# Grouped attention in a decoder trunk: the weighted sums in two products, with values' main part and remainder side by side

## The chip, the cores and the metric

The kernel runs on one core of a Trainium2 chip. The metric is the device time of one execution in microseconds (us); lower is better. A core has a matrix engine (TensorE, PE in the profile, with its weight loads shown as PEld), a vector engine (VectorE, DVE), a scalar engine (ScalarE, ACT), GpSimd (POOL) and SyncE (SP). TensorE writes its results to PSUM; the other data lie in SBUF. Both are memories of 128 partitions, and an instruction works on the same columns of many partitions at once.

## The reference

The reference is a decoder trunk of four layers over 256 positions of width 2048. Each layer normalizes its input, projects it, mixes the positions, multiplies by a gate, projects back and adds. The mixers cycle: latent attention, sparse attention over selected keys, sliding-window attention with sinks, latent attention again. The change touches the second and the third, which both are grouped: 32 query heads share 4 key and value heads, 8 to a group, of width 64. Cut to the lines that matter:

```python
# sparse layer (selected keys)
s = jnp.einsum('bqgjd,bqkgd->bqgjk', qb, kg, preferred_element_type=jnp.float32) * B_HEAD_DIM ** -0.5 + bias
p = jax.nn.softmax(s, axis=-1)
return jnp.einsum('bqgjk,bqkgd->bqgjd', p.astype(vg.dtype), vg)
...
# sliding-window layer
s = jnp.einsum('bqgjd,bkgd->bgjqk', qb, kb, preferred_element_type=jnp.float32) * scale + bias
p = e / (jnp.sum(e, axis=-1, keepdims=True) + jnp.exp(sink - m))
return jnp.einsum('bgjqk,bkgd->bqgjd', p.astype(vb.dtype), vb)
...
# both
y = jnp.concatenate([self_out, mem_out], axis=-1) * jax.nn.silu(gate)
x = x + y @ w_out[i]
```

The last `einsum` of each mixer is the weighted sum of values. All inputs are 32-bit floats.

## The kernel before

**Numbers in two parts.** Most matrix products are done on a rounded 32-bit type (`F32R`). To keep accuracy an operand is split into a main part and a remainder: `split` (L67) lets ScalarE copy the value into the rounded type (L60) and VectorE subtract that copy from the value (L69). A product of two split operands is three matmuls: main by main, main by remainder, remainder by main.

**The projections.** Weights come from memory by SyncE's queue into buffers `wr`; `parts_of` (L233) splits each 512-column piece into `wh` and `wl`, with three buffers of each. `rows_by` (L239) uses such a piece in six products of 512 columns (L264, L265, L266, for two row blocks), `columns_by` (L269) in four of 512 (L284) and four of 256 (L288). ScalarE makes `wh`, VectorE `wl`, TensorE uses both.

**Order.** The program is written as one sequence. A scheduler that simulates the engines decides in which order each engine gets its instructions, under the data dependencies; each engine then runs its own list strictly in order and waits on semaphores. A few instructions are pinned to the written order. Tiles with the same tag share a fixed number of buffers. PSUM tiles from `misc` (tag `mp`) share four; the score tiles `sp`, the transposed weights `tp`, the indexer's tiles and the sums `o` are among them.

**Grouped attention.** `Grouped.first` projects keys and values and, in the sliding-window layer, calls `spaced_values` at once. In the sparse layer an indexer (`select`, `stacked_late`, `selection`) runs first, in steps between other work, and `spaced_values` follows at its end. `stacked_late` contains, at L841 and L843, a copy from the upper to the lower half of the partitions on ScalarE and an addition on VectorE.

`spaced_values` (L766) writes the values of the four groups, 64 columns each, into two zeroed tiles `vz[0]` (main part, tag `big1`) and `vz[1]` (remainder, tag `big2`) of 9 x 64 columns per key block, with 64 zero columns between them. GpSimd zeroes them (L772).

`Grouped.attend` (L902) works on one group of 8 heads in the order 0, 2, 1, 3, 4, 6, 5, 7. For each head two query blocks of 128 are scored, put through a softmax and transposed: three 128 x 128 blocks, since the first query block sees one key block and the second sees two. The transposed weights are split into `pHL[0]` and `pHL[1]`. Two even heads (or two odd heads) fill one such pair of tiles. After the second of them come the weighted sums (L940), called one event here: for key block `t` = 0, 512 columns of weights (two blocks of two heads), for `t` = 1, 256 columns, and for each the three products. The 128 columns of `vz` that serve as the other operand begin at the values for even heads and 64 columns earlier for odd heads, so that the sums of even heads land in partitions 0 to 63 and those of odd heads in 64 to 127, and zeros are added to the other half. The even and the odd event add into one PSUM tile `o`. After the odd one VectorE multiplies `o` by the gate (L946) into `yt`, a tile of a kind with three buffers, and `yt` is split into `y`.

A layer runs its parts in the order 4, 0, 1, 2, 3, 5 (4 and 5 are attention to the memory); the output projection `w_out` of a part is written after the next part's attention. One layer has 4 groups with 4 events each.

Of the kernel before, what the change touches and what calls it, by code (L numbers as in the profile page):

```python
# [9 lines left out]
F32R = mybir.dt.float32r  # L10
I32 = mybir.dt.int32
AF = mybir.ActivationFunctionType
# [3 lines left out]
P = 128  # L16
S = 256
# [14 lines left out]
def kernel(ctx: ExitStack, tc: tile.TileContext, a: dict, out: bass.AP,  # L32
                             kinds=(0, 1, 2, 0)):
    nc = tc.nc
# [3 lines left out]
    act = ctx.enter_context(tc.tile_pool(name="act", bufs=1))  # L38
# [4 lines left out]
    def misc(name, dt=F32):  # L43
        return ps.tile([P, 512], dt, name=name, tag="mp", bufs=4)

    def tmp(name, n=512, dt=F32):
        return wk.tile([P, n], dt, name=name, tag=f"t{n}", bufs=3)
# [5 lines left out]
    def f32(ap):  # L53
        return ap.bitcast(F32)
# [4 lines left out]
    def copy_act(o, i, scale=1.0):  # L59
        inst = nc.scalar.activation(o, i, AF.Copy, scale=scale)  # L60
        if pinned:
            tc.keep_in_program_order(inst)
# [4 lines left out]
    def split(hi, lo, src):  # L67
        copy_act(hi, src)
        nc.vector.tensor_sub(lo, src, f32(hi))  # L69
# [158 lines left out]
    def other_work():  # L228
        for _ in range(2):
            if steps and next(steps[0], None) is None:  # L230
                steps.pop(0)
# [268 lines left out]
    def attend(o, v, pT):  # L500
        nc.tensor.matmul(o, v[0], pT[:, :S], start=True, stop=False)
        nc.tensor.matmul(o[:, P:], v[1], pT[:, S:S + P], start=False, stop=True)
# [109 lines left out]
    class Latent:  # L612
# [101 lines left out]
        def attend(self, qn, qr, kn, v, gT):  # L714
            y = act.tile([P, 2, 4, S], F32R, name="y", tag="y", bufs=2)
            for h in range(4):
                def score(b):
                    sp = misc("sp")
                    qs = slice(b * P, (b + 1) * P)
                    q, k, z = qn[h // 2], kn[h // 2], h % 2  # L720
                    if b == 0:
                        seq = [(q[:, 0, z, qs], k[:, :, z, :P]), (q[:, 1, z, qs], k[:, :, z, :P]),
                               (qr[:, h, qs], self.kr[:, :, :P])]
                    else:
                        seq = [(q[:, 0, z, qs], k[:, 0, z, :]), (q[:, 0, z, qs], k[:, 1, z, :]),
                               (q[:, 1, z, qs], k[:, 0, z, :]),
                               (qr[:, h, qs], self.kr[:, 0, :]), (qr[:, h, qs], self.kr[:, 1, :])]
                    for n_, (l, r_) in enumerate(seq):
                        nc.tensor.matmul(sp[:, :S], l, r_, start=n_ == 0, stop=n_ == len(seq) - 1)
                    return sp  # L730
                tp = masked_softmax(score, lambda b, n: caus[:, S - n:], self.scale)
                pT = wk.tile([P, 768], F32, name="pT", tag="pT", bufs=PT)[:, :512]
                copy_act(pT[:, :3 * P], tp[:, :3 * P])
                if h % 2 == 0:
                    o = misc("o")
                attend(o[:, (h % 2) * S:(h % 2 + 1) * S],
                       [v[:, t, h * P:(h + 1) * P] for t in range(2)], pT)
                if h % 2 == 1:
                    gated(y, o, gT, h - 1)
            return y  # L740


    class Grouped:
# [22 lines left out]

        def spaced_values(self):


            self.vz = [act.tile([P, 2, 9 * 64], F32R, name="vz", tag=f"big{1 + z}") for z in range(2)]  # L770
            for z in range(2):
                nc.gpsimd.memset(f32(self.vz[z]), 0.0)  # L772
            for t in range(2):
                hi, lo = (self.vz[z][:, t, 64:].rearrange("p (g c) -> p g c", c=P)[:, :, :64] for z in range(2))
                split(hi, lo, self.v[:, t, :].rearrange("p (g c) -> p g c", c=64))

        def dup(self, dst, src, sc, n):

# [123 lines left out]
        def attend(self, g, q, bm, gT):  # L902
            while steps:
                other_work()
            y = act.tile([P, 2, 4, S], F32R, name="y", tag="y", bufs=2)
            for h in (0, 2, 1, 3, 4, 6, 5, 7):
                def score(b):
                    sp = misc("sp")
                    qb = q[h // 4][:, h % 4, b * P:(b + 1) * P]
                    if b == 0:  # L910
                        nc.tensor.matmul(sp[:, :S], qb, self.k[:, g, :, :P], start=True, stop=True)
                    else:
                        for v in range(2):
                            nc.tensor.matmul(sp[:, :S], qb, self.k[:, g, v, :],
                                             start=v == 0, stop=v == 1)
                    return sp

                def bias(b, n):
                    bh = bm[:, h, S - n:]
                    if not self.sparse:  # L920
                        return bh
                    bs = wk.tile([P, S], F32, name="bs", tag="e", bufs=4)
                    nc.vector.tensor_add(bs[:, :n], bh, self.sel[:, b, :n])
                    return bs[:, :n]
                nsk = None if self.sparse else nsink[:, g * 8 + h:g * 8 + h + 1]
                tp = masked_softmax(score, bias, None, nsk)

                half, odd = h // 2 % 2, h % 2
                if half == 0:
                    pHL = [wk.tile([P, 3, 2, P], F32R, name="pT2", tag="pT", bufs=PT) for z in range(2)]  # L930
                split(pHL[0][:, :, half, :], pHL[1][:, :, half, :],
                      tp[:, :3 * P].rearrange("p (i c) -> p i c", i=3))
                if half == 0:
                    continue
                if not odd:
                    o = misc("o")
                v0 = g * P + (0 if odd else 64)
                for t in range(2):
                    for n_, (z, p_) in enumerate(((0, 0), (0, 1), (1, 0))):
                        nc.tensor.matmul(o[:, t * S:], self.vz[z][:, t, v0:v0 + P],  # L940
                                         pHL[p_][:, 2 * t:2 + t].rearrange("p i h c -> p (i h c)"),
                                         start=odd == t == n_ == 0, stop=odd == t == 1 and n_ == 2)
                if odd:
                    j = (h // 4) * 2
                    yt = tmp("yt")
                    nc.vector.tensor_mul(yt.rearrange("p (j b c) -> p j b c", j=2, b=2),  # L946
                                         o.rearrange("p (b j c) -> p j b c", b=2, j=2),
                                         gT[:, j:j + 2, :].rearrange("p j (b c) -> p j b c", b=2))
                    split(y[:, 0, j:j + 2, :], y[:, 1, j:j + 2, :], yt.rearrange("p (a b) -> p a b", a=2))
            return y  # L950

# [129 lines left out]
```

## Time and profile before

| | |
|---|---|
| runs of the kernel | 2596.93, 2597.0, 2600.05 us; median 2597.0 |
| the profiled execution | 2597.13 us |
| its span, first to last instruction | 2595.3 us |
| mean granted TensorE clock | 0.998 |
| bytes moved by DMA | 509.53 MB |
| matmuls | 14066 |

The profile is one execution, recorded by the hardware. Its page gives the busy time of each engine, the span in 40 slices, the chain of work that ended last, and the costliest groups of instructions. A group's row names line, engine, operation, tiles (output, arrow, inputs), shape and count; behind the bar stand the busy time in us, the mean duration of one in ns, and the idle time of the engine just before, with what ended it. Further views of the same execution give the waits, a timeline, or busy times by windows. Durations of matmuls that follow each other overlap, so the time that one takes from the span is the distance between starts.

### The profile page before, as it was taken

To read this page: it belongs to the slowest core of one execution; us is meant where nothing else is said; L and a number is where in the kernel's file an instruction comes from. 1 tells how busy PE (TensorE), PEld (TensorE's weight loads), DVE (VectorE), ACT (ScalarE), POOL (GpSimd) and SP (SyncE) were. 2 spreads that over 40 slices of the span, in tenths; PEclk is the share of its full clock that TensorE was granted. 3 is DMA by queue.
4 is the path that set the end of the run, shared out by engine and by line. 5 is a ranking of instruction groups with operands and counts; after the bars stand their busy time and mean duration, and the time that the engine had idled before them with its cause. 6 is when DMAs were issued, how large, how long until landed. Compare 5 with 4: busy or idle time off the path is not lost.

```text
span 2595.3 us, 41702 instructions
## 1 busy us (share of the span) xinstructions
PE 2576.4 (99%) x14066; PEld 2216.7 (85%) x14066; DVE 1880.5 (72%) x4130; ACT 1619.6 (62%) x3420; POOL 68.0 (3%) x124
## 2 busy tenths in 40 slices
PE   9999999999999999999999999999999999999997
PEld 7888898888888888888888888888888888888886
DVE  7666667667776686787778776777778767676667
ACT  6556556556656566667666666676666655665655
POOL 0100000000000010000000000000000000000000
PEclk9999999999999999999999999999999999999999
DMA  7888777666676667566556575555655766566664
GB/s 257 254 258 267 242 214 234 185 171 190 193 203 201 197 218 246 163 196 189 192 164 199 170 224 170 175 174 180 195 161 149 233 183 168 170 167 182 212 178 131
DMA packets 455128, 509.53 MB, mean 196 GB/s; under 512 B 68816, under 2 KB 351712, under 8 KB 453760
## 3 DMA queue, kind: packets, MB, share of 16 engines
q1 hardware_dynamic: 441392, 449.58, 57.9%
q0 software_dynamic: 13088, 56.16, 6.8%
q8 instruction: 110, 1.80, 0.3%
q10 hardware_dynamic: 432, 1.11, 0.1%
q14 instruction: 106, 0.87, 0.1%
HBM read 487.81 MB, written 31.56 MB: 200 GB/s over the span
## 4 chain that ended last, share of the span: by engine, by line
PE 99%; DVE 1%; ACT 0%; DMA 0%; SPq 0%; issue 0%; ACTq 0%
PE acc_g L284 14%; PE acc_g L288 7%; PE acc_wo L264 7%; PE acc_wo L265 7%; PE acc_wo L266 7%; PE acc_mk L284 5%; PE acc_mq L284 5%; PE acc_cq L284 3%; PE acc_qn L284 3%; PE acc_mq L288 2%; PE acc_mk L288 2%; PE acc_q L265 2%; PE acc_q L266 2%; PE acc_q L264 2%; PE acc_mv L265 2%; PE acc_mv L264 2%
## 5 line engine op out<-in xcount | busy, mean ns | idle before, releaser
L69 DVE TENSOR_TENSOR wl<-wr,wh 128x512 fp32r<-128x512 f32 (+2 forms) x1728 | 1165.0, 677 | 625.8 <-ACT wh L60 602.8
L60 ACT ACTIVATE wh<-wr 128x512 fp32r<-128x512 f32 (+2 forms) x1728 | 1070.4, 621 | 813.8 <-PE acc_g L284 179.3
L284 PE MATMUL acc_g<-xT,wh 128*128 128x512 f32 x1536 | 486.3, 396 | 0.0
L288 PEld LDWEIGHTS acc_g<-xT,wl 128*128 128x128 f32 x1536 | 284.8, 188 | 60.8
L288 PE MATMUL acc_g<-xT,wl 128*128 128x256 f32 x1536 | 310.5, 280 | 0.0
L265 PE MATMUL acc_wo<-wl,y 128*128 128x512 f32 x768 | 303.5, 395 | 0.2 <-DVE wl L69 0.2
L266 PE MATMUL acc_wo<-wh,y 128*128 128x512 f32 x768 | 298.2, 390 | 0.0
L284 PEld LDWEIGHTS acc_g<-xT,wh 128*128 128x128 f32 x1536 | 238.3, 189 | 4.4
L264 PE MATMUL acc_wo<-wh,y 128*128 128x512 f32 x768 | 240.1, 391 | 0.1
L265 PEld LDWEIGHTS acc_wo<-wl,y 128*128 128x128 f32 x768 | 144.3, 188 | 28.4 <-DVE wl L69 0.6
L266 PEld LDWEIGHTS acc_wo<-wh,y 128*128 128x128 f32 x768 | 144.3, 188 | 27.9
L264 PEld LDWEIGHTS acc_wo<-wh,y 128*128 128x128 f32 x768 | 142.2, 188 | 29.2 <-ACT y L60 1.0
L284 PE MATMUL acc_mk<-mT,wh 128*128 128x512 f32 x512 | 161.7, 396 | 0.3 <-DVE mv L418 0.3
L284 PE MATMUL acc_mq<-xT,wh 128*128 128x512 f32 x512 | 161.6, 396 | 0.0
L968 DVE TENSOR_TENSOR x<-x,acc_wo 128x512 f32<-128x512 f32 x192 | 126.1, 681 | 5.7 <-PE acc_wo L266 5.6
L284 PE MATMUL acc_qn<-cT,wh 128*128 128x512 f32 x384 | 121.2, 397 | 0.0
L284 PE MATMUL acc_cq<-xT,wh 128*128 128x512 f32 x384 | 120.8, 396 | 0.0
L288 PEld LDWEIGHTS acc_mk<-mT,wl 128*128 128x128 f32 x512 | 96.0, 188 | 22.3 <-DVE wl L69 0.4
L288 PEld LDWEIGHTS acc_mq<-xT,wl 128*128 128x128 f32 x512 | 94.0, 188 | 20.1
L288 PE MATMUL acc_mq<-xT,wl 128*128 128x256 f32 x512 | 103.3, 282 | 0.0
L288 PE MATMUL acc_mk<-mT,wl 128*128 128x256 f32 x512 | 101.9, 278 | 0.0
L265 PE MATMUL acc_q<-wl,xT 128*128 128x512 f32 x256 | 101.1, 395 | 0.0
(304 smaller groups left out, 4272.5 us busy)
## 6 DMA issues: line engine op xcount, KB each, us to landing
wr<-in_w_out_dram SPq DMA_DIRECT2D x192, 512.0 KB, 3.6
wr<-in_w_in_a_dram SPq DMA_DIRECT2D x176, 512.0 KB, 4.0
wr<-in_w_mem_kv_dram SPq DMA_DIRECT2D x120, 512.0 KB, 4.4
wr<-in_w_in_b_dram SPq DMA_DIRECT2D x112, 512.0 KB, 3.5
wr<-in_w_in_c_dram SPq DMA_DIRECT2D x104, 512.0 KB, 3.5
wr<-in_w_uq_dram SPq DMA_DIRECT2D x192, 128.0 KB, 2.5
wr<-in_w_uq_dram SPq DMA_DIRECT2D x48, 256.0 KB, 3.7
tab<-flat POOLq DMA_DIRECT2D x8, 1536.0 KB, 9.4
```

Source lines behind the costliest of these rows:

```text
L60: inst = nc.scalar.activation(o, i, AF.Copy, scale=scale)
L69: nc.vector.tensor_sub(lo, src, f32(hi))
L264: nc.tensor.matmul(acc[t][:, :n], xh, wh[:, :n], start=first, stop=False)
L265: nc.tensor.matmul(acc[t][:, :n], xh, wl[:, :n], start=False, stop=False)
L266: nc.tensor.matmul(acc[t][:, :n], xl, wh[:, :n], start=False, stop=last)
L284: nc.tensor.matmul(acc[j], wh[:, o:o + P], q[:, :, kt % 4, :], start=kt == 0, stop=False)
L288: nc.tensor.matmul(acc[j][:, 0, :], wl[:, o:o + P], q[:, 0, kt % 4, :], start=False, stop=kt == kts - 1)
L968: nc.vector.tensor_add(xs, xs, acc[t])
```

## The change

The diff touches `spaced_values` and the end of `Grouped.attend`.

- There is one tile of spaced values, in tag `big2`. A group has 192 columns: 64 zeros, the 64 values' main parts, their 64 remainders.
- An event has two products for each key block. The first multiplies the main part of the weights by the columns main, remainder: partitions 0 to 63 get main by main, 64 to 127 get remainder by main. The second multiplies the remainder of the weights by the columns zeros, main: it adds main by remainder into partitions 64 to 127.
- Each event has its own tile `o`. The two halves are added across partitions: ScalarE copies the other half of `o` into this head pair's half of `yt`, and VectorE adds this half of `o`. Even heads end in partitions 0 to 63 of `yt`, odd heads in 64 to 127, as before.
- The product with the gate reads `yt` and writes `yt`, where it read `o`.

```diff
         def spaced_values(self):
 
-
-            self.vz = [act.tile([P, 2, 9 * 64], F32R, name="vz", tag=f"big{1 + z}") for z in range(2)]
-            for z in range(2):
-                nc.gpsimd.memset(f32(self.vz[z]), 0.0)
-            for t in range(2):
-                hi, lo = (self.vz[z][:, t, 64:].rearrange("p (g c) -> p g c", c=P)[:, :, :64] for z in range(2))
-                split(hi, lo, self.v[:, t, :].rearrange("p (g c) -> p g c", c=64))
+            self.vz = act.tile([P, 2, 4 * 192], F32R, name="vz", tag="big2")
+            nc.gpsimd.memset(f32(self.vz), 0.0)
+            for t in range(2):
+                v3 = self.vz[:, t, :].rearrange("p (g c) -> p g c", c=192)
+                split(v3[:, :, 64:128], v3[:, :, 128:], self.v[:, t, :].rearrange("p (g c) -> p g c", c=64))
...
                 if half == 0:
                     continue
+
+
+                o = misc("o")
+                for t in range(2):
+                    for p_ in range(2):
+                        c0 = g * 192 + 64 * (1 - p_)
+                        nc.tensor.matmul(o[:, t * S:], self.vz[:, t, c0:c0 + P],
+                                         pHL[p_][:, 2 * t:2 + t].rearrange("p i h c -> p (i h c)"),
+                                         start=t == p_ == 0, stop=t == p_ == 1)
                 if not odd:
-                    o = misc("o")
-                v0 = g * P + (0 if odd else 64)
-                for t in range(2):
-                    for n_, (z, p_) in enumerate(((0, 0), (0, 1), (1, 0))):
-                        nc.tensor.matmul(o[:, t * S:], self.vz[z][:, t, v0:v0 + P],
-                                         pHL[p_][:, 2 * t:2 + t].rearrange("p i h c -> p (i h c)"),
-                                         start=odd == t == n_ == 0, stop=odd == t == 1 and n_ == 2)
+                    yt = tmp("yt")
+                here, other = (slice(64, P), slice(0, 64)) if odd else (slice(0, 64), slice(64, P))
+                oj = o.rearrange("p (b j c) -> p j b c", b=2, j=2)
+                yj = yt.rearrange("p (j b c) -> p j b c", j=2, b=2)
+                nc.scalar.activation(yj[here], oj[other], AF.Copy)
+                nc.vector.tensor_add(yj[here], yj[here], oj[here])
                 if odd:
                     j = (h // 4) * 2
-                    yt = tmp("yt")
-                    nc.vector.tensor_mul(yt.rearrange("p (j b c) -> p j b c", j=2, b=2),
-                                         o.rearrange("p (b j c) -> p j b c", b=2, j=2),
-                                         gT[:, j:j + 2, :].rearrange("p j (b c) -> p j b c", b=2))
+                    nc.vector.tensor_mul(yt, yt, gT[:, j:j + 2, :].rearrange("p a b -> p (a b)"))
                     split(y[:, 0, j:j + 2, :], y[:, 1, j:j + 2, :], yt.rearrange("p (a b) -> p a b", a=2))
```

## The prediction

> **What bounds the kernel now.** I read the page first: the busy times, the clock in the slices, the chain that ended last.
>
> ```profile
> span 2595.3 us, 41702 instructions
> ## 1 busy us (share of the span) xinstructions
> PE 2576.4 (99%) x14066; PEld 2216.7 (85%) x14066; DVE 1880.5 (72%) x4130; ACT 1619.6 (62%) x3420; POOL 68.0 (3%) x124
> ...
> PEclk9999999999999999999999999999999999999999
> ...
> PE 99%; DVE 1%; ACT 0%; DMA 0%; SPq 0%; issue 0%; ACTq 0%
> ```
>
> TensorE (PE) is busy for 99% of the span at full clock, and 99% of the chain is matmuls. A busy PE need not be a PE at its limit, because matmuls overlap. So I asked next where the changed products lie, then what PE waited for in that stretch, then how loaded the other engines are there. The first row below is the tile view of the spaced values (shortest, median, longest ns; first and last start). The next six are all of PE's waits over the span (us in total, times, longest); cut to 1160 to 1940 us, the same view keeps the rows of `o` and `acc_wo` alone. The last two are windows that hold one layer's changed products each: length, then busy time of PE, PEld, DVE, ACT and POOL, clock, DMA share, GB/s.
>
> ```profile
> L940 PE MATMUL o<-pT,vz x192: 277/336/496, 1163.5 to 1936.8; 128*128 128x512 f32 x96, 128*128 128x256 f32 x96
> ```
>
> ```profile
> PE spr L175 <- DVE dg L174: 2.6, 1, 2.6
> PE wu L101 <- DVE ones L97: 1.1, 1, 1.1
> PE acc_mv L264 <- ACT wh L60: 1.1, 2, 0.6
> PE o L940 <- DVE pT L69: 0.3, 1, 0.3
> PE acc_mk L284 <- DVE mv L418: 0.3, 1, 0.3
> PE acc_wo L265 <- DVE wl L69: 0.2, 1, 0.2
> ```
>
> ```profile
> 1160.00:1545.00 385.00, 384.76 (x2062) 327.83 (x2061) 300.91 (x702) 256.92 (x576) 10.89 (x17) 1.00 0.60 188
> 1620.00:1940.00 320.00, 319.60 (x1705) 270.86 (x1705) 245.34 (x614) 218.39 (x533) 3.79 (x5) 1.00 0.57 178
> ```
>
> In 780 us PE waited 0.5 us. VectorE (DVE) has 84 and 75 us free in the two windows, ScalarE (ACT) 128 and 102 us. Here the number of matmul columns sets the time, so columns taken out come off the span unless what replaces them makes PE wait.
>
> **The products that go.** The grouped view gives the number of products by form; a piece of the chain holds one event whose six products stand together, and what follows them.
>
> ```profile
> L940 PE MATMUL o<-pT,vz 128*128 128x512 f32 x96 | 32.5, 400 | 0.3 <-DVE pT L69 0.3
> L940 PE MATMUL o<-pT,vz 128*128 128x256 f32 x96 | 16.5, 280 | 0.0
> L940 PEld LDWEIGHTS o<-pT,vz 128*128 128x128 f32 x192 | 33.2, 188 | 6.5 <-DVE pT L69 0.8
> ```
>
> ```profile
> 1182.41 1.05 PE o L940 x6
> 1183.46 0.46 PE acc_q L264 x2
> ```
>
> The 192 products are 32 events of six (2 layers, 4 groups, 4 pairs of heads): three of 512 columns, three of 256. The change leaves two of each, so 64 products go, with their weight loads. The means of 400 and 280 ns overlap and are not the price. The chain is: six take 1.05 us, from 1182.41 to the next product at 1183.46. A 512-column product takes 0.46 / 2 = 0.23 us there, which leaves (1.05 - 3 x 0.23) / 3 = 0.12 us for one of 256. An event loses 0.23 + 0.12 = 0.35 us, 32 events lose 11.2 us. A weight load takes 188 ns and yet these products follow each other after 0.12 us, so loads overlap and add nothing to the price.
>
> The Trainium skill gives, for a stream of weight loads and matmuls in a real kernel, about 81 ns a matmul at 128 columns and 131 ns at 512 (TensorE: Matmul & The Clock Gate, Back-to-back issue gap). By that, as an estimate, an event would lose between 0.131 + 0.081 and 0.131 + 0.131 us, and the sum would be 6.8 to 8.4 us. The row of 1.05 us for six disagrees: by the page's figures six would take 0.64 to 0.79 us.
>
> **What comes in.** Each event now ends in a ScalarE copy of 64 x 512 out of PSUM, from the other half of the partitions, and a VectorE add of 64 x 512 with one operand in PSUM. The first of the two layers does just such a pair once, in its indexer (L841, L843). The product with the gate stays, but reads SBUF where it read PSUM.
>
> ```profile
> L841 ACT ACTIVATE lo<-acc_iq 64x512 f32<-64x512 f32 x1 | 0.6, 595 | 0.3 <-PE acc_iq L262 0.3
> L843 DVE TENSOR_TENSOR zq<-lo,acc_iq 64x512 f32<-64x512 f32 x1 | 0.7, 678 | 0.4 <-ACT lo L841 0.4
> L69 DVE TENSOR_TENSOR y<-yt,y 128x512 fp32r<-128x512 f32 x48 | 32.9, 685 | 6.9 <-ACT y L60 6.9
> L946 DVE TENSOR_TENSOR yt<-o,gT 128x512 f32<-128x512 f32 x16 | 11.0, 687 | 1.4 <-PE o L940 0.6
> ```
>
> ScalarE gets 32 x 0.595 = 19.0 us more, VectorE 32 x 0.678 = 21.7 us more; the gate's product stays at 0.69 us (685 from SBUF, 687 from PSUM). Per event that is 0.6 us against 128 / 16 = 8.0 and 102 / 16 = 6.4 us of free ScalarE time, and 0.68 us against 84 / 16 = 5.3 and 75 / 16 = 4.7 us on VectorE. So I cost it at nothing; what hides it is that free time. Copies from the low to the high half (the odd heads) have no row; I take 595 ns for them too; at twice that they would still fit into the 6.4 us.
>
> The waits are the open part. The copy waits for the event's last product. Behind it in ScalarE's order stands, in 24 of 32 places, the exponential of the next head's softmax, then the copies that make `wh`. The add waits for the copy; behind it on VectorE stand softmax steps and the subtractions that make `wl`. PE waits for `wh`, `wl` and, for the next event, the weights `pT`. How far is it covered? These rows of the first window show who holds up ScalarE.
>
> ```profile
> ACT wh L60 <- PE acc_wo L266: 28.0, 39, 1.3
> ACT wh L60 <- PE acc_g L284: 21.5, 34, 1.4
> ACT wh L60 <- PE acc_q L266: 14.5, 16, 1.8
> ```
>
> In 89 cases ScalarE waited for PE to free a `wh` buffer: it runs as far ahead as three buffers let it. One buffer feeds six products of 0.23 us, 1.4 us; with two waiting ahead, PE does not feel a delay below 2.8 us. Copy and add in a row are 1.27 us. Below: the one PE wait in such an event, the last of the second layer, could vanish, as its `pT` may come in time. Its start is 0.73 us after the product before, 0.5 us more than 0.23.
>
> ```profile
> 1935.24 0.40 PE L940 MATMUL o<-pT,vz 128*128 128x512 f32 x1
> 1935.97 1.08 PE L940 MATMUL o<-pT,vz 128*128 128x512 f32 x5 [0.34 <-DVE pT L69]
> ```
>
> Above: such a 0.5 us at each of the 32 events would give back 16 us. The value I take is 0, because the list of PE's waits has one such event in 32.
>
> PSUM: each event now takes a buffer of its own, but gives it back after copy and add, where before one was held from the even heads' products over a whole further pair of softmaxes. `yt` is now held from the even event on, one of three buffers; the others who use them in these layers are the memory part's `yt` and the next norm's tiles at a layer's end. I cost both at 0, with the bounds of the waits above.
>
> The zeroing of the spaced values becomes one fill instead of two, of 1536 columns instead of 1152.
>
> ```profile
> L772 POOL MEMSET vz<- x4: 1062/1063/1068, 1083.5 to 1453.2; 128x1152 f32 x4
> ```
>
> By size it takes 1.4 us where two took 2.1. It still waits for the last indexer product in the first layer, and for the first layer's last event in the second. The first use at 1163.5 comes 80 us after the first fill, and the second fill at 1453 lies far ahead of the second layer: cost 0. No DMA is added, and SyncE's order is the same. On POOL it now stands wholly behind a load of memory values that stood between the two fills before.
>
> The scheduler also reorders. PE's order is the same for its first 6,076 products and its last 3,307; in between, score and transpose steps move by some tens of products against the projections. I cost that at 0 with up to 4 us above (next part).
>
> **Sum.** The profiled execution took 2597.13 us (span 2595.3 and 1.8 around it); the median shown is 2597.0, so it stands for the runs. 2597.1 - 11.2 + 0 = 2585.9, say 2586 us.
>
> **Rivals.** (1) Part of it comes back. After a group's last event its output `y` is 1.27 us later, and a changed order can put a product in front of its operand. At the price of the one wait seen, 0.5 us, in each of 8 groups: 4 us, 2590 us. For it: that wait stands in a group's last event. Against it: `y` is used only after the next part's attention.
>
> (2) The change does not pay: another engine or the weight stream takes over as the bound, and the time stays near 2597. For it: VectorE is 77 to 78% busy in the windows and gets 3% more; DMA share is 0.57 to 0.60. Against it: PE waits 0.5 us in 780 and never for a DMA there.
>
> (3) Slower. Draining the products becomes the limit: the copy stands at the head of ScalarE's order waiting for PE while PE has no tile ahead, so PE stands for copy and add, 1.27 us at each event, 40.7 us in all: 2597.1 - 11.2 + 40.7 = 2626.6 us. It decides against the change from 0.35 us of PE wait per event on. For it: both new steps wait in strict order with `wh` and `wl` work behind them. Against it: the same pair at L841 and L843 waited 0.3 and 0.4 us and PE's list has no wait of the indexer's; 2.8 us of tiles lie ahead. [...]
>
> **How the numbers follow.** Forecast (2584 to 2588) 0.70; rival 1 (2588 to 2592) 0.12; rival 2 (2592 to 2602) 0.09; rival 3 (above 2602) 0.09. A change of 0.2% is 5.2 us, about what a measurement here can tell from none. Faster by more, below 2591.8: 0.70 + 0.12 = 0.82; within: 0.09; slower: 0.09. For the range I go from 2583.5 (the 11.2 us, the vanished 0.5, and 2 us for runs that spread: 2596.93 to 2600.05 before) to 2592, the end of rival 1; that leaves out 0.18.
>
> **What would show it.** PE's products 14066 - 64 = 14002; six-product runs of 1.05 us become four of 0.70; PE busy lower by about 11 us; new rows of 0.6 us on ScalarE and 0.68 us on VectorE, 32 each; PE's waits between 1160 and 1940 us still below 2 us. It is wrong if PE's waits for `wl`, `wh` or `pT` rise to several us, if four products take more than 0.8 us, or if a stretch outside the two layers changes its length.

## The result, and the profile after

The changed kernel takes 2620.3 us (median of 6 runs, 2618.75 to 2621.43); the kernel before took 2598.5 us beside it (6 runs, 2596.93 to 2600.05). The ratio is 1.0083, with a 95% interval of 1.0073 to 1.0093. The change makes the kernel slower by 22 us; the prediction was 11 us faster.

The page of the changed kernel, whose profiled execution took 2618.75 us, shows the products gone and the new work there (14002 products, 32 more instructions on VectorE and ScalarE), and yet a longer span. The last row shown is the chain of work that ended last, in which TensorE had 99% before:

```profile
span 2617.0 us, 41603 instructions
PE 2579.7 (99%) x14002; PEld 2211.0 (84%) x14002; DVE 1902.4 (73%) x4162; ACT 1637.8 (63%) x3452; POOL 66.6 (3%) x122
...
PE 96%; ACT 2%; DMA 1%; DVE 1%; issue 0%; SPq 0%; ACTq 0%; DVEq 0%
```

The grouped view, shapes apart, gives the new instructions their durations:

```profile
L939 PE MATMUL o<-pT,vz 128*128 128x512 f32 x64 | 26.2, 410 | 0.5 <-ACT pT L60 0.5
L939 PE MATMUL o<-pT,vz 128*128 128x256 f32 x64 | 12.6, 279 | 0.0
L947 ACT ACTIVATE yt<-o 64x512 f32<-64x512 f32 x32 | 19.0, 592 | 7.6 <-PE o L939 6.9
L948 DVE TENSOR_TENSOR yt<-yt,o 64x512 f32<-64x512 f32 x32 | 21.9, 683 | 3.5 <-ACT yt L947 3.3
L951 DVE TENSOR_TENSOR yt<-yt,gT 128x512 f32<-128x512 f32 x16 | 10.9, 684 | 0.1
```

The copy takes 592 ns and the add 683 ns, as the prediction had them from the indexer's pair (595 and 678). So nothing new is dear in itself. The same two windows as before, and then TensorE's waits from 1160 to 1965 us, a stretch that holds all of this kernel's changed products:

```profile
1160.00:1545.00 385.00, 377.72 (x1990) 317.30 (x1989) 306.89 (x709) 263.33 (x588) 9.69 (x15) 1.00 0.58 182
1620.00:1940.00 320.00, 311.03 (x1613) 260.13 (x1612) 246.57 (x596) 217.67 (x518) 3.79 (x5) 0.99 0.55 173
```

```profile
PE acc_wo L264 <- ACT wh L60: 8.5, 12, 1.0
PE tr L465 <- DVE hl L795: 5.4, 8, 1.4
PE acc_wo L264 <- ACT y L60: 2.4, 2, 1.6
PE acc_wo L264 <- DVE z L295: 1.5, 3, 0.5
PE o L939 <- ACT pT L60: 0.5, 3, 0.2
PE ptp L497 <- ACT e L60: 0.4, 1, 0.4
```

Before, TensorE waited 0.5 us in the two layers; now it waits 18.7 us (8.5 + 5.4 + 2.4 + 1.5 + 0.5 + 0.4). Almost none of that is at the changed products (`o`, 0.5 us), and no wait names the copy or the add. TensorE waits for other steps: split weights `wh`, parts `hl` of the queries, the output `y`. They lie at the ends of the groups, between 3.6 us before a group's last event and 7.7 us after it. This is the timeline around one of them (start, duration, engine, line; in brackets the idle time before and what ended it):

```profile
1706.24 0.50 PE L264 MATMUL acc_wo<-wh,y 128*128 128x512 f32 x1 [0.50 <-DVE z L295]
...
1707.75 0.81 PE L497 MATMUL ptp<-ident,e 128*128 128x128 f32 x3
...
1709.16 0.51 PE L264 MATMUL acc_wo<-wh,y 128*128 128x512 f32 x1 [0.60 <-ACT wh L60]
...
1711.35 0.63 PE L939 MATMUL o<-pT,vz 128*128 128x512 f32 x3
...
1712.15 0.59 ACT L947 ACTIVATE yt<-o 64x512 f32<-64x512 f32 x1
...
1712.77 0.69 DVE L948 TENSOR_TENSOR yt<-yt,o 64x512 f32<-64x512 f32 x1 [0.61 <-ACT yt L947]
...
1714.13 0.50 PE L465 MATMUL tr<-identr,hl 128*128 128x128 f32 x4 [1.38 <-DVE hl L795]
```

Within 8 us the last head's softmax, transposes and event, the gate and the next group's query parts come together, and TensorE stands three times for 0.5 us or longer. What has to be explained is why they come together there. TensorE's busy time rose all the same, by 3.3 us over the span (2576.4 to 2579.7) although 64 products went, so it doesn't measure the work done here.

**Where to look next.** The order of TensorE's products shows a difference in the middle of a group, where nothing waits yet. This is the same place in both kernels, the event of the odd heads 1 and 3 of a group, on TensorE alone; `sp` are the scores of the next head. First the kernel before:

```profile
1736.44 0.36 PE L911 MATMUL sp<-kd,qS 128*128 128x256 f32 x1
...
1741.45 0.40 PE L940 MATMUL o<-pT,vz 128*128 128x512 f32 x1
...
1742.39 0.98 PE L940 MATMUL o<-pT,vz 128*128 128x512 f32 x5
```

The changed kernel:

```profile
1753.85 0.40 PE L939 MATMUL o<-pT,vz 128*128 128x512 f32 x1
1754.09 0.28 PE L909 MATMUL sp<-kd,qS 128*128 128x256 f32 x1
```

Before, the next head's scores start 5.0 us ahead of the event (1741.45 - 1736.44). After, they start 0.24 us behind the event's first product. All 8 such events show it: 4.3 to 5.0 us ahead in the one kernel, 0.24 us behind in the other. At the even events the scores start 0.24 us behind in both. The next head's softmax, which runs on VectorE and ScalarE, so begins some 5 us late, once in every group.

### The profile page after: what moved, and what is told of

Same layout as the page of the kernel before. It is cut to its first block, busy times and chain, and to the rows that moved or that the text cites. A ratio compares the mean times of both kernels' runs of the same rounds, so it can differ in the third digit from the quotient of the medians.

```text
span 2617.0 us, 41603 instructions
## 1 busy us (share of the span) xinstructions
PE 2579.7 (99%) x14002; PEld 2211.0 (84%) x14002; DVE 1902.4 (73%) x4162; ACT 1637.8 (63%) x3452; POOL 66.6 (3%) x122
## 4 chain that ended last, share of the span: by engine, by line
PE 96%; ACT 2%; DMA 1%; DVE 1%; issue 0%; SPq 0%; ACTq 0%; DVEq 0%
PE acc_g L284 13%; PE acc_g L288 7%; PE acc_wo L264 7%; PE acc_wo L265 6%; PE acc_wo L266 6%; PE acc_mk L284 5%; PE acc_mq L284 5%; PE acc_cq L284 3%; PE acc_qn L284 3%; PE acc_mq L288 2%; PE acc_mk L288 2%; PE acc_q L265 2%; PE acc_q L266 2%; PE acc_q L264 2%; PE acc_mv L265 2%; PE acc_mv L264 2%
## 5 line engine op out<-in xcount | busy, mean ns | idle before, releaser
L266 PE MATMUL acc_wo<-wh,y 128*128 128x512 f32 x768 | 297.5, 391 | 0.0
L264 PE MATMUL acc_wo<-wh,y 128*128 128x512 f32 x768 | 246.6, 398 | 12.5 <-ACT wh L60 8.5
```

The source lines that it names most:

```text
L264: nc.tensor.matmul(acc[t][:, :n], xh, wh[:, :n], start=first, stop=False)
L266: nc.tensor.matmul(acc[t][:, :n], xl, wh[:, :n], start=False, stop=last)
```

## Experiments

All kernels below were timed beside the kernel before, which took 2598.5 to 2599.5 us. Each diff is against the kernel named.

### The change taken apart

Four kernels separate the products, the copy and add, and the PSUM tile. In their expectations W is the theory that copy and add hold up TensorE through ScalarE's and VectorE's strict order, T that the tile of its own per event does it, O that any change of the program reorders enough.

**Products alone**, changed kernel without copy and add, one tile for both events. The odd heads' sums are added onto the even heads', main parts in one half of the tile and remainders in the other, so the sums are not those of the reference.

```diff
-                o = misc("o")
+                if not odd:
+                    o = misc("o")
...
-                nc.scalar.activation(yj[here], oj[other], AF.Copy)
-                nc.vector.tensor_add(yj[here], yj[here], oj[here])
```

> Two products instead of three, but one PSUM tile for an even and an odd event as before, and neither the copy nor the add (the halves are not added, so the sums lack a part). 64 products fewer, nothing more on ScalarE and VectorE. If copy and add cost the time (theory W), or the tile of its own per event does (theory T): 2598.5 - 11.2, about 2587 us. If taking out products alone makes the scheduler choose a worse order (theory O): above 2600 us.

Measured: 2591.5 us, ratio 0.9969 (0.9957 to 0.9980). O falls; the gain is 7.5 us of the 11.2.

**Copy, add and own tile without the saving**: the changed kernel with the three products and the two spaced-value tiles of before, so that the copied half is zero.

> Three products as before, but each event has its own PSUM tile, and copy and add follow it (they add a half of zeros). W and T both: 2598.5 + 33, about 2631 us (the changed kernel's 2620 plus the 11.2 us of products). O: anything, with no reason to be slower than 2598.5 by the same 33.

Measured: 2624.7 us, ratio 1.0096 (1.0081 to 1.0111), slower as W and T both say, but 6 us short of their 2631: beside own tiles, copy and add the products are worth only 4.4 us (2624.7 - 2620.3).

**One tile**: the changed kernel, all its work kept; only the odd event writes into the tile that the even event has been read from.

```diff
-                o = misc("o")
+                if not odd:
+                    o = misc("o")
```

> The changed kernel with one change: an even and an odd event share one PSUM tile, taken at the even event, as before; copy and add stay. T: the loss goes, about 2587 us. W: it stays, 2620 us. If both count, in between, and the split shows how much each does.

Measured: 2599.7 us, ratio 1.0001 (0.9991 to 1.0010).

**Own tiles in the kernel before**: a tile for each event, and so the gate's product in two halves of 64 partitions (16 more VectorE instructions); no copy, no add.

```diff
-                if not odd:
-                    o = misc("o")
+                o = misc("o")
...
+                here = slice(64, P) if odd else slice(0, 64)
+                nc.vector.tensor_mul(yt.rearrange("p (j b c) -> p j b c", j=2, b=2)[here],
+                                     o.rearrange("p (b j c) -> p j b c", b=2, j=2)[here],
+                                     gT[:, j:j + 2, :].rearrange("p j (b c) -> p j b c", b=2)[here])
```

> The kernel before with a PSUM tile of its own for each event and the gate's product taken in two halves (one more VectorE instruction of 64 x 512 per pair, 11 us of its time in all); no copy, no add, three products. T: about 2630 us. W: about 2598 to 2605 us.

Measured: 2615.7 us, ratio 1.0062 (1.0047 to 1.0077), between the two expectations. At all 8 events of the odd heads 1 and 3 the next head's scores now start 0.24 us behind the event's first product, as in the changed kernel; in the kernel with one tile they start 3.9 to 5.0 us ahead of it.

The one line that gives the odd event a tile of its own is worth 2620.3 - 2599.7 = 20.7 us. In the kernel before, without any of the new work, own tiles cost 16.7 us (with 11 us of gate product more on VectorE). W alone predicted 2620 us for one tile and falls. T predicted 2587 us there and falls short by 13: with one tile the change still only breaks even. The products alone give 7.5 us, so copy and add take about 8 (2599.7 - 2591.5).

### Is it the order, and is it where the tile is written?

Tiles of `misc` share four buffers. My theory (S): buffers of a tag are handed out in the written order. In the changed kernel the odd event's `o` is written ahead of the next head's scores, so the scores can't take a buffer until the event does, and the event waits for the weights of its second head. In the kernel before that `o` had been taken at the even event already, and the scores went ahead.

**Written late**: the changed kernel, two tiles as before, but the odd event is put down in the program behind the next head's scores (at a group's end, behind the next group's query parts).

```diff
+                def weigh(odd=odd, h=h, pHL=pHL):
+                    nonlocal yt
+                    o = misc("o")
...
+                if odd:
+                    late.append(weigh)
+                else:
+                    weigh()
...
                             nc.tensor.matmul(sp[:, :S], qb, self.k[:, g, v, :],
                                              start=v == 0, stop=v == 1)
+                        flush()
```

> The changed kernel with every event still in a PSUM tile of its own; only the place changes where the odd heads' event (its four products, copy, add, gate product) is written down: behind the next head's score products, or at a group's end behind the next group's query parts, instead of ahead of them. Slot theory (S): PSUM tiles of the shared tag are handed out in written order, so in the changed kernel the next head's score cannot start before the odd event has its tile; written later, the event no longer stands in front of it, and the cost of the own tile (20.7 us from one shared tile to two) mostly goes: 2597 to 2604 us. Room theory (R): one more tile is alive in a tag of four and everybody waits for room: then the written place does not matter, 2615 to 2622 us.

Measured: 2604.1 us, ratio 1.0019 (1.0010 to 1.0028). Its TensorE timeline at the same event as above:

```profile
1744.06 0.36 PE L917 MATMUL sp<-kd,qS 128*128 128x256 f32 x1
...
1749.10 0.40 PE L950 MATMUL o<-pT,vz 128*128 128x512 f32 x1
...
1750.04 0.63 PE L950 MATMUL o<-pT,vz 128*128 128x512 f32 x3
```

The scores are back 5.0 us ahead of the event (3.9 to 5.0 at the 8 places), and 16.2 of the 20.7 us are back too, with the number of tiles unchanged; that is the upper end of what S expected. The run moves both odd events of a group at once, the one in the middle and the one at the end, and doesn't tell what each place is worth. The rival, that one more live tile leaves the others too little room, said 2615 to 2622 us and falls.

**The kernel before in the changed kernel's order**: its work and its one tile unchanged, with its instructions on TensorE, ScalarE and VectorE tied into the changed kernel's order.

> The kernel before, its work unchanged (three products, one shared tile, no copy and add), with its instructions on TensorE, ScalarE and VectorE forced into the order of the changed kernel. If the order alone carries the loss of the own tile: 2612 to 2622 us, like the kernel before with own tiles (2615.7). If the loss comes from the new work or from PSUM itself: 2597 to 2604 us.

Measured: 2622.8 us, ratio 1.0092 (1.0076 to 1.0107). TensorE's waits:

```profile
PE acc_wo L264 <- ACT wh L60: 7.0, 12, 0.8
PE tr L465 <- DVE hl L797: 3.1, 6, 0.7
...
PE acc_wo L264 <- ACT y L60: 2.1, 2, 1.3
PE acc_wo L264 <- DVE z L295: 1.5, 3, 0.5
```

The same waits on the same operands appear without any new work. The order carries the loss (2622.8 lies just above the expected 2622), and by the runs with one tile and with own tiles a PSUM tile carries most of the order. Which of the many moves in that order cost what is not shown.

### What copy and add cost

**Copy without add**: one tile; ScalarE copies the main part's half, the remainder is left out of the sums.

```diff
-                nc.scalar.activation(yj[here], oj[other], AF.Copy)
-                nc.vector.tensor_add(yj[here], yj[here], oj[here])
+                nc.scalar.activation(yj[here], oj[here], AF.Copy)
```

> The changed kernel with one shared tile, without the add: ScalarE copies the half with the main part, the remainder's half is left out of the sums. ScalarE keeps its 19 us of new work, VectorE has none of the adds. If the adds on VectorE are the cost: 2590 to 2594 us, as with products alone (2591.5). If the copy on ScalarE is: 2597 to 2601 us, as with both (2599.7).

Measured: 2591.0 us, ratio 0.9969 (0.9957 to 0.9981), the same as the products alone. The 19 us of copies on ScalarE cost nothing; the adds cost 8.7 us.

**The same work in the order of before**: one tile, copy and add, tied into the order of the kernel before, with copy and add right behind their event.

> The changed kernel with one shared tile (2599.7 us by itself), its instructions forced into the order of the kernel before, with copy and add put in right behind their event. If the 8 to 9 us of copy and add come only from the order that the scheduler chooses around them: 2588 to 2593 us. If they come from the work itself, in any order: 2597 to 2605 us.

Measured: 2597.6 us, ratio 0.9993 (0.9984 to 1.0003). It takes back 2.1 of the 8.7 us, and the two kernels' intervals overlap; the second expectation holds, that the cost comes from the work itself.

**The copy on VectorE** (`nc.vector.tensor_copy` in place of the activation), one tile.

> The changed kernel with one shared tile, the copy done by VectorE instead of ScalarE, so that ScalarE has no new work and there is no hand-over between the two engines. If copy and add cost by standing in ScalarE's order ahead of softmax and wh: faster than 2599.7, 2590 to 2596 us. If they cost by VectorE's time (77% busy in the layer) : slower, 2601 to 2610 us.

Measured: 2621.9 us, ratio 1.0089 (1.0074 to 1.0104), 22.2 us slower than with the copy on ScalarE and slower than either expectation. The tile view gives what went to VectorE, 32 x 688 ns = 22.0 us:

```profile
L948 DVE COPY yt<-o x32: 683/688/693, 1166.9 to 1963.2; 64x512 f32<-64x512 f32 x32
```

So VectorE's time seemed to be the price, although VectorE stood free for 75 to 84 us in each window. The next runs take time off it.

**Gate product on GpSimd** (`nc.gpsimd.tensor_mul`), one tile; and **gate product and remainder of `y` on GpSimd**; and, as a control, **the kernel before with the remainder of `y` on GpSimd**.

> The changed kernel with one shared tile, and the product with the gate, which since the change reads SBUF alone, moved from VectorE to GpSimd: 16 instructions of 0.69 us, 11 us, leave VectorE. If what is left of the cost of copy and add is VectorE's time (21.9 us of adds cost 8 us; a copy moved there cost 22): 2590 to 2596 us, below the kernel before. If VectorE's time isn't it, or GpSimd's longer product holds up y: 2598 to 2606 us.

Measured: 2598.2 us, ratio 0.9997 (0.9989 to 1.0006).

> As the run with the gate product on GpSimd, and the subtraction that makes the remainder of y there too: 22 us leave VectorE, as much as the adds brought. VectorE's time as the cause: 2587 to 2593 us. Otherwise, or if y comes too late through GpSimd's two steps in a row: 2598 to 2610 us.

Measured: 2602.3 us, ratio 1.0009 (1.0000 to 1.0018).

> The kernel before, with only the subtraction that makes the remainder of y (16 of 0.69 us in the two layers) on GpSimd: does less work on VectorE pay without the change too? If VectorE has no price there (PE waits 0.5 us in 780): 2596 to 2601 us, as before. If VectorE's time is a price at any load: 2590 to 2595 us.

Measured: 2601.8 us, ratio 1.0012 (1.0003 to 1.0021). Three times the expectation fails that less work on VectorE pays: 11 us off VectorE gave 1.4, 22 us off it lost 2.6, and in the kernel before 11 us off it lost 2.7. The first two differences lie within the intervals, the third just outside. The product itself takes twice as long there (0.69 us on VectorE):

```profile
L952 POOL TENSOR_TENSOR yt<-yt,gT 128x512 f32<-128x512 f32 x16 | 21.8, 1362 | 547.7 <-DVE yt L949 547.7
```

Either VectorE's time has no fixed price, or GpSimd's longer steps give back what it brings; these runs can't part the two.

**One add a pair**: ScalarE copies main part and remainder of both events, VectorE adds once, 128 x 512.

```diff
+                nc.scalar.activation(zj[here], oj[here], AF.Copy)
                 nc.scalar.activation(yj[here], oj[other], AF.Copy)
-                nc.vector.tensor_add(yj[here], yj[here], oj[here])
...
+                    nc.vector.tensor_add(yt, yt, zm)
```

> The changed kernel with one shared tile; ScalarE copies main part and remainder of each event into SBUF (64 copies instead of 32, 19 us more on ScalarE), and VectorE adds once a pair, 128x512, instead of twice 64x512: 16 adds instead of 32, 11 us less on VectorE. If the cost of copy and add goes with the adds (copy alone 2591.0, with 32 adds 2599.7): 2593 to 2597 us, below the kernel before. If it is the later sums, or ScalarE's second copy costs what the first did not: 2598 to 2604 us.

Measured: 2601.4 us, ratio 1.0008 (0.9999 to 1.0016). Half the adds, no gain. The run changes two more things: ScalarE has 19 us more to do, and the second tile `zm` takes another of the three buffers of `yt`'s kind.

**Idle copy**: the kernel without the add, plus a VectorE copy of 64 x 512 from the event's tile that nobody reads.

> The run without the add (2591.0 us) with a VectorE copy of 64x512 out of the event's PSUM tile put in, whose result nobody reads; it waits for the event's products, as the add does, but nothing waits for it. If the add costs by taking VectorE's time at that place: 2597 to 2602 us. If it costs because the gate product and y come later behind copy and add: 2590 to 2593 us.

Measured: 2595.7 us, ratio 0.9986 (0.9977 to 0.9995): 4.7 us for 22 us of VectorE's time that nobody waits for, between the two expectations. The tile that it writes is of `yt`'s kind too, so beside VectorE's time it takes one of those three buffers at each event.

**Free adds**: in its place an add of two SBUF operands, once of the residual `x` into a scratch tile, once of the bias tile's used slices in place.

> As the run with the idle copy, but the instruction put in is an add of 64x512 of two SBUF tiles that are there long before, so that it can stand anywhere in VectorE's order; its result is read by nobody. If VectorE's time costs wherever it is spent: 2597 to 2602 us. If the add costs only because it has to stand in order behind the event: 2590 to 2593 us.

Measured: 2632.7 us, ratio 1.0128 (1.0112 to 1.0143). This add wasn't free: the residual's own adds wait behind it, and TensorE for them.

```profile
PE acc_g L284 <- DVE hl L795: 10.0, 3, 3.3
PE acc_q L264 <- DVE x L973: 4.5, 6, 0.9
```

> The run without the add (2591.0 us) with an add of 64x512 put in at each event that works in place on the bias tile of the two heads just read, in SBUF: it waits for no product and nothing reads it, and no residual add comes behind it, as it did with the free add on the residual (2632.7, where TensorE waited for the residual's adds). If VectorE's time costs wherever it stands, like the idle copy (2595.7): 2594 to 2598 us. If only an instruction that has to wait for the event costs: 2590 to 2593 us.

Measured: 2605.4 us, ratio 1.0027 (1.0016 to 1.0037), 14.4 us for the same time on VectorE, more than either expectation. It is not free of followers either. The next group's load of the bias table goes into the same buffer, and by the tile view of `bm` it waited for this add in 6 of 8 cases:

```profile
who waited for it (us, times):
  POOL bm L896: 501.0, 6
```

In the kernel without the add these 6 loads wait for the tile's last reader. What the later load adds is not shown; but none of the three runs with an extra instruction spends VectorE's time alone.

**The adds of one half of the events left out** (with their remainders): first those of each group's second pair of events, then those of the first.

```diff
-                nc.scalar.activation(yj[here], oj[other], AF.Copy)
-                nc.vector.tensor_add(yj[here], yj[here], oj[here])
+                add = h < 4
+                nc.scalar.activation(yj[here], oj[other if add else here], AF.Copy)
+                if add:
+                    nc.vector.tensor_add(yj[here], yj[here], oj[here])
```

> The changed kernel with one shared tile, without the adds of each group's second pair of events (16 of 32; their remainders are left out of the sums). In the kernel before VectorE is 90% busy in the 16 us behind a group's last event and 74% between groups. If the adds cost where VectorE is already full, at the group's end: 2591 to 2594 us, as without any add (2591.0). If every add costs the same: 2594.5 to 2596.5 us.

Measured: 2597.3 us, ratio 0.9992 (0.9983 to 1.0001).

> The other half: without the adds of each group's first pair of events, with those at the group's end. If the adds cost at the group's end: 2597 to 2600 us, as with all adds (2599.7). If every add costs the same: 2594.5 to 2596.5 us.

Measured: 2598.8 us, ratio 0.9999 (0.9990 to 1.0008). The first fits neither of its expectations; the second fits the group's end, but there the first should have gained the rest. One half taken away gives 2.4 us, the other 0.9, both together 8.7. The costs don't add. The intervals are as wide as these differences, but the length of a layer tells more: the first layer, which the change doesn't touch, takes 595.9 or 596.0 us in all 20 profiled executions. By layer, measured in the traces from the first key and value product of the layer to that of the next layer:

| kernel, one tile | sparse layer, us | sliding-window layer, us |
|---|---|---|
| without adds | 533.8 | 479.0 |
| adds of the first pair only | 534.1 | 484.5 |
| adds of the second pair only | 536.9 | 483.2 |
| all adds | 536.7 | 484.2 |

In the sparse layer the second pair's adds cost all of the 2.9 us. In the sliding-window layer the first pair's adds alone cost 5.5 us and the second's 4.2, and both together no more, 5.2. Where VectorE is loaded is seen in the kernel before (windows: length, then busy time of PE, PEld, DVE, ACT and POOL; the first and last begin at a group's last event):

```profile
1702.00:1718.00 16.00, 16.00 (x82) 13.24 (x81) 13.86 (x37) 12.26 (x30) 0.00 (x0) 1.00 0.56 178
1718.00:1756.00 38.00, 38.00 (x191) 31.66 (x190) 28.27 (x70) 24.70 (x60) 0.00 (x0) 1.00 0.55 171
1777.00:1793.00 16.00, 16.00 (x80) 13.29 (x80) 14.55 (x38) 11.47 (x30) 0.00 (x0) 1.00 0.52 158
```

At a group's end VectorE is busy 87 and 91% (13.86 and 14.55 of 16 us), between them 74%. The 77% that I had read for the whole window is a mean over these. That fits a price for work on VectorE, but the runs don't show how much of it is the load at the group's end: leaving out the adds there brought the gain in the sparse layer (534.1 us) and not in the other (484.5).

No version with the whole sums is clearly below the kernel before; the nearest is one tile in the order of before, 0.9993 with an interval that holds 1.

## Why the prediction was wrong, step by step

The sign was wrong. Summed by the runs: products 2591.5 - 2599.0 = -7.5 us, copy 2591.0 - 2591.5 = -0.5, adds 2599.7 - 2591.0 = +8.7, own tile 2620.3 - 2599.7 = +20.7. Together +21.4, against 2620.3 - 2598.5 = +21.9 measured.

- **The step that failed** is PSUM: "each event now takes a buffer of its own, but gives it back after copy and add ... I cost both at 0". I looked at how long a buffer is held, and at the event alone. What counted was when the buffer is asked for, and who stands behind it in the written order: the next head's scores. The next sentence of that kind fell with it, "The scheduler also reorders ... I cost that at 0 with up to 4 us above". I had seen score steps move and not asked why they moved. Sixteen of the 20.7 us came back when only the written place changed; the order alone, forced on the old work, costs 23 us (2622.8).
- **The products** were priced rightly and counted on too fully. In the kernel with products alone, the chain shows four together:

```profile
1182.69 0.70 PE o L940 x4
1183.39 0.46 PE acc_q L264 x2
```

  It is 0.70 us, 0.35 less than the six, as predicted. The Trainium skill's spacing for a stream of loads and products (TensorE: Matmul & The Clock Gate, Back-to-back issue gap) would make it 0.42 to 0.52 us as an estimate, two of 131 ns and two of 81 to 131; the row disagrees here too. Of 32 x 0.35 = 11.2 us, 7.5 arrived. Most of the rest came back as waits, which is the size of the first rival (2590 us): TensorE's waits at the output projection are 2.4 us in that kernel (1.4 + 0.5 + 0.5), where the list of before has 0.2:

```profile
PE acc_wo L265 <- DVE wl L69: 1.4, 4, 0.6
PE acc_wo L264 <- ACT wh L60: 0.5, 1, 0.5
PE acc_wo L264 <- ACT y L60: 0.5, 1, 0.5
```

  The traces take the time apart further, by the distances between the starts of TensorE's products from the first key and value product of the sparse layer to that of the last layer. The usual distance is the median in the kernel before: 230 ns behind a product of 512 columns, 116 behind 256, 84 behind 128. What goes beyond it stands under "waits" if the next product, or the one before it, had waited, and under "half clock" where the granted clock was 0.50.

| kernel | the two layers, us | usual distances | waits | half clock | rest |
|---|---|---|---|---|---|
| before | 1020.8 | 1007.9 | 1.7 | 0.0 | 11.2 |
| products alone | 1012.4 | 996.8 | 4.5 | 0.0 | 11.2 |
| one tile | 1020.9 | 996.8 | 11.9 | 0.0 | 12.3 |
| changed | 1042.3 | 998.2 | 28.0 | 3.0 | 13.1 |

  So the products did come off in full (1007.9 - 996.8 = 11.1 us). What the change gives back, and more, are losses at waits; the half clock is told at the end. The changed kernel's 998.2 holds 1.4 us of products that the other three do behind the last layer's first product, and its last layer is shorter by as much (596.4 us, 597.8 before); the prediction had named a changed length outside the two layers as a sign of being wrong.
- **The copy** at 0 was right: 592 ns in both directions across the partitions (588 to 597 for all 32), and in the run without the add, where it stays within its half, hidden in ScalarE's free time.
- **The add** at 0 was wrong: 8.7 us. The step was "So I cost it at nothing; what hides it is that free time". Free time by the mean of a window was not free time where the work fell due; that fits VectorE's 87 to 91% at the groups' ends, though the runs with half the adds don't prove it. The 2.8 us of `wh` tiles ahead, which were to cover a delay, didn't: at the output projection TensorE waits 4.5 us for `wh` with one tile and 8.5 us in the changed kernel, where the kernel before has no such wait.
- **The fill** and `yt` held longer: the fill takes 1.38 us, as forecast by its size (1.4). The kernels with products alone and with copy alone contain the new fill, and the latter the longer `yt`; they gained 7.5 and 8.1 us. Neither step was isolated; nothing in these runs needs a cost for them.
- **The rivals.** The third gave 2626.6 us and lies close, but its mechanism isn't what happened: TensorE doesn't stand at each event for copy and add (waits at `o` are 0.5 us in all), and the same loss is there without them. What the new steps cost went by their engine: nothing for the copy on ScalarE, 8.7 us for the add on VectorE, 22.2 us more with the copy on VectorE too.

**What stays open.** Why equal time on VectorE costs 4.7, 8.7, 14.4 or 22.2 us by place is not settled. Each such kernel is also scheduled anew, and order alone moved the same work by 2.1 us (2599.7 to 2597.6) with one tile. The granted clock differs too: with the copy on VectorE and with the adds on the residual it was 0.50 for 13.7 and 17.1 us of the sparse layer, which lost 5.6 and 7.2 us there, and nowhere in the two layers with the idle copy or the adds on the bias tile. An add that reads both halves from PSUM at once, which would need no copy, was not tried, nor were the adds with a hand-written order. Of the own tile's 20.7 us, 4.5 remain when the event is written late (2604.1 - 2599.7). There the losses at waits, counted as in the table, are 16.2 us against 11.9 with one tile, and TensorE's waits for `y` are 4.2 us against 1.0: `y`, written later too, comes too late for the output projection.

## What to carry to other kernels

A tile that shares a rotating tag has a place in the written order; if a change lets a step take its own tile where it used an older one, look at who takes the next tile of that tag, and expect that step to start no earlier. When the order of instructions moves by tens on the engine that sets the time, find the cause before costing it at nothing. Read the free time of a second engine where the new work falls due, not as a mean over the layer, and measure half of a suspected cost as well as all of it: here the halves didn't add up.

## What the hardware showed beside this

The length of a VectorE instruction went by its columns here, not by its partitions: the add of 64 x 512 takes 683 ns, the gate's product of 128 x 512 takes 684 ns, and with one operand in PSUM or none it is the same. The partitions that an instruction leaves unused are lost, which is why two half adds cost as much as two whole ones. And a wait costs TensorE more than its idle time. The product at 1706.24, behind a wait of 0.50 us, starts 0.89 us after the one before it, where 0.23 us is the rule, and the next follows after 0.34 us: 0.77 us are lost.

```profile
1705.35 0.39 PE L266 MATMUL acc_wo<-wh,y 128*128 128x512 f32 x1
...
1706.24 0.50 PE L264 MATMUL acc_wo<-wh,y 128*128 128x512 f32 x1 [0.50 <-DVE z L295]
...
1706.58 0.40 PE L265 MATMUL acc_wo<-wl,y 128*128 128x512 f32 x1
...
1706.82 0.40 PE L266 MATMUL acc_wo<-wh,y 128*128 128x512 f32 x1
```

The granted clock dropped as well. In the changed kernel's profiled execution it was 0.50 for 3.4 us from 1795.6 us, and again from 1877.6 us, each time 0.6 us after the product that ended a wait of 1.38 us; 512-column products then start 0.43 us apart. The first stretch as a window (its clock is the 0.50), and two products from its timeline:

```profile
1795.60:1799.00 3.40, 3.40 (x11) 2.71 (x10) 2.72 (x10) 2.62 (x8) 0.00 (x0) 0.50 0.00 0
...
1796.23 0.63 PE L265 MATMUL acc_wo<-wl,y 128*128 128x512 f32 x1
1796.66 0.63 PE L266 MATMUL acc_wo<-wh,y 128*128 128x512 f32 x1
```

Waits of 1.38 us at 1714.13 and 1.56 us at 1961.28 had no such stretch behind them, so that a wait brings it on is not shown. The kernel before has none in the two layers, and neither has that kernel in the changed kernel's order, which loses as much (2622.8 us): the clock adds to the loss and is not its cause.
